# An MLP by seven products on one Trainium2 core: another order of products, three accumulators, other places for the first factors and the last outputs

## The chip, the cores and the metric

The kernel runs on one core of one Trainium2 chip. The metric is the device time of one execution in microseconds; a change of less than about 0.2% can't be told from none.

## The reference

One inference step of a decoder layer for 1024 prompt tokens and 8 samples that share the weights: pooling mixer and gated linear attention in parallel, output projection, cross-attention to memory tokens, and an MLP. The change lies in the MLP and behind it:

```python
    hf = _rmsnorm(x, norm_ffn_g)
    a = jax.nn.relu(jnp.einsum('btd,df->btf', hf, w_up))
    x = x + jnp.einsum('btf,fd->btd', a * a, w_down)
...
    y_prompt = _rmsnorm(xp, norm_final_g)
    y_sample = _rmsnorm(xs, norm_final_g)
```

with D_MODEL = 1024 and D_FF = 4096. All is float32.

## The kernel before

**Arithmetic.** A float32 matrix is split into two parts, `hi` (a cast to fp32r on ScalarE, L157) and `lo` (a subtraction on VectorE, L158), and a matmul is done as three: hi x hi, hi x lo, lo x hi. The two matrix products of the MLP are done by blocks of 2x2, with seven block products in place of eight; the factors are sums and differences of blocks. On the way up a tile m (0 to 15) holds 128 rows of each half of the hidden units. Tokens are in halves of 512 (prompt) and 520 (prompt and samples); products on 520 columns are two matmuls of 260 each.

**Way up.** `first_products(m)` does products 1 and 2 for all 16 m, adds them up, squares the relu, and stores block b11 to DRAM (`fd["2"][m]`); product 1 stays in `P1` (a slot for four m). Then `other_products(m)` does products 4, 6, 5, 7, 3 for each m. Its weights are one tile `w4` (four loads on SyncE, L1131), combined in place on VectorE (L1140 to L1143, `s1` being a tile of its own). Product 7 goes on in the accumulator of product 6, so L1155, which adds `P1` to what stands there, must come before it; product 3 goes on in that of product 5 in the same way (the copy in L1158). L1160 to L1164 add up the results, relu and square follow on ScalarE, and L1172 to L1181 form the factors of the way down, partly in the storage of `w4`; ScalarE and GpSimd store them to DRAM (`fd["1"]`, `fd["3"]` to `fd["7"]`). The b11 block that they need is loaded back (L1135).

**Way down.** `DOWN` lists seven products in the order 2, 3, 1, 6, 5, 4, 7. For each of four m and two halves q, `down_w` loads a weight block (raw `wdn`), splits it into `wdnh` and `wdnl`, `down_part` does the matmuls (L1275), and `factor` loads and splits a factor of the next product, so that eight factors F are there when it begins. For product 2 five factors are made during the loop on the way up (`first_factor`, after m = 2, 4, 5, 9, 13), three at the change to the way down.

**The end.** Product 7 is last. Its last two row blocks are done in column halves (`last_part`); `finish(t)` transposes 128 tokens, takes the norm (L1315, square and sum on ScalarE) and scales (L1318) and stores; the last two token blocks (`ys`, `junk`, `last_sum`) are normed piece by piece, with a last scaling in L1409.

**What sets the order.** A scheduler puts the instructions in order, engine by engine, from the dependences and from the program's order as priority; every engine then runs its list in order, and DMA issues on a queue go in order too. Buffers come from pools: `slot()` gives one of 19 shared slots of a tile pool S (`w4`, `P1`, the split inputs T, F, X), `T()` one of four temporary buffers (`c12` with b11, `c2`, `fac`, `y`), `wp` the raw weights and their split parts. The eight PSUM banks hold two single-bank tiles `mp` and two accumulators of three banks each on the way up; on the way down `mp` has two and `accp` three of two banks. A tile that gets a buffer waits for the last user of the tile that had it.

Of the kernel before, what the change touches and what calls it, by code (L numbers as in the profile page):

```python
# [16 lines left out]
P = 128  # L17
# [43 lines left out]
def body(ctx, tc, a, o):  # L61
# [11 lines left out]
    mp = front.enter_context(tc.tile_pool(name="mp", bufs=2, space=PSUM))  # L73
    accp = front.enter_context(tc.tile_pool(name="accp", bufs=2, space=PSUM))
# [110 lines left out]
    def gemm_steps(src, X, name, cols=ALL):  # L185

        W = src if isinstance(src, list) else load_w(src, name)
        acc = accp.tile([P, NG, 512], F32, tag="acc", name="acc")
# [62 lines left out]
    def tokens_sum(ss, name):  # L251

        pt = accp.tile([P, NG, 512], F32, tag="acc", name="pts")
# [102 lines left out]
    def x_chunk(k):  # L356
        xT = T("xT")
        acc = accp.tile([P, NG, 512], F32, tag="acc", name="ptx")
# [20 lines left out]
    def f_part(k):  # L379
        if k == 0:  # L380
            FW.append(accp.tile([P, NG, 512], F32, tag="acc", name="accf"))
        for j in range(2):
            for g in range(NG):
                PE.matmul(FW[KC][:, g, :GS], FW[k], H[k][j][:, g * GS:(g + 1) * GS],
                          start=(k == 0 and j == 0), stop=(k == KC - 1 and j == 1))
# [70 lines left out]
    def forget():  # L456
# [3 lines left out]
        for p in range(2):  # L460
            acc = accp.tile([P, NG, 512], F32, tag="acc", name="accz")
# [57 lines left out]
    def pool_out(gi):  # L519
# [6 lines left out]
        acc = accp.tile([P, NG, 512], F32, tag="acc", name="accp")  # L526
# [119 lines left out]
    def gla1(c):  # L646
        cs = slice(c * P, (c + 1) * P)
        acc = GA[c] = accp.tile([P, NG, 512], F32, tag="acc", name="accg")
# [297 lines left out]
    def scores(h, tt):  # L946
        acc = accp.tile([P, NG, 512], F32, tag="acc", name="accsc")
# [22 lines left out]
    def context(h, tt):  # L970
        pT = PT.pop((h, tt))
        acc = accp.tile([P, NG, 512], F32, tag="acc", name="accpv")
# [53 lines left out]
    def norm(half):  # L1026
# [3 lines left out]
        pt = accp.tile([P, NG, 512], F32, tag="acc", name="pts3")  # L1030
# [83 lines left out]
    def first_products(m):  # L1114
        acc = accp.tile([P, NG, 512], F32, tag="acc", name="acc12")
# [11 lines left out]
    def other_products(m):  # L1127
# [6 lines left out]
        G.memset(b11[:, HA:], 0.0)  # L1134
        SY.dma_start(b11[:, :HA], fd["2"][m])  # L1135
# [14 lines left out]

        d = mp.tile([P, 512], F32, tag="m", name="acc4")
        product([(d, 0, HA)], w_split(w4[:, 3]), "4")
        va, ta = both(accp.tile([P, NG, 512], F32, tag="acc", name="acc67"))
        product(ta, w_split(w4[:, 0]), "6")
        V.tensor_tensor(out=g2(c12), in0=va, in1=g2(p1), op=ALU.add)  # L1155
        vc, tc_ = both(accp.tile([P, NG, 512], F32, tag="acc", name="acc53"))
        product(tc_, w_split(s1), "5")
        A.copy(out=g2(c22), in_=vc)  # L1158
# [25 lines left out]
    run(ATTN)  # L1184
    for half in range(2):
# [15 lines left out]
    def first_factor(j):  # L1201

        ff = slot([P, 2, 2, HA], F32R, "F2")
        for k in range(2):
            t = wp.tile([P, HA], F32, tag="raw", name="fac2", bufs=3)
            SY.dma_start(t, fd["2"][2 * j + k])
            split(ff[:, 0, k], ff[:, 1, k], t)
        F.setdefault("2", []).append(ff)

    for m in range(MU):  # L1210
        other_products(m)
        if m in (2, 4, 5, 9, 13):
            first_factor(len(F.get("2", [])))
# [9 lines left out]
    mp = ctx.enter_context(tc.tile_pool(name="mpd", bufs=2, space=PSUM, reuse_waits="tile"))  # L1223
    accp = ctx.enter_context(tc.tile_pool(name="accpd", bufs=3, space=PSUM, reuse_waits="tile"))
# [14 lines left out]
    def factor(n, j):  # L1239

        w = width(n)
        t = T("fac", 2 * w).rearrange("p (k n) -> p k n", k=2)
        SY.dma_start(t, fd[n][2 * j:2 * j + 2].rearrange("k p n -> p k n"))
        ff = slot([P, 2, 2, w], F32R, "F" + n)
        split(ff[:, 0], ff[:, 1], t)
        F.setdefault(n, []).append(ff)

    def down_w(n, blocks, op, m, q, keep=False):

        raw = []  # L1250
# [9 lines left out]
        if keep:  # L1260
            w = slot([P, 2, UK, P], F32R, "wd")
            hi, lo = w[:, 0], w[:, 1]
        else:
            hi = wp.tile([P, UK, P], F32R, tag="whi", name="wdnh", bufs=2)
# [175 lines left out]
```

## Time and profile before

| | |
|---|---|
| time, median of 3 runs | 1395.98 us (1395.47 to 1396.54) |
| the profiled execution, its own time | 1395.87 us |
| span, first to last instruction | 1394.2 us |
| TensorE busy | 1328.1 us (95%) |
| VectorE busy | 918.6 us (66%) |
| ScalarE busy | 578.9 us (42%) |
| GpSimd busy | 135.3 us (10%) |
| mean granted TensorE clock | 0.983 |

Busy time leaves out what an engine spends on register, branch, semaphore and DMA-issuing instructions. The span is some 1.7 us shorter than the execution's own time; the latter is compared with the median. The granted clock is a share of full speed, 2.4 GHz; 0.50 is the lower of its two levels, 1.2 GHz.

### The profile page before, as it was taken

The page shows a single profiled execution, that of the slowest core. Times are in us where ns is not written, and L with a number is a line of the kernel's source. Part 1 is how long each engine was busy: PE and PEld are TensorE (multiplying, and loading weights), DVE is VectorE, ACT ScalarE, POOL GpSimd, SP SyncE. Part 2 cuts the span into 40 slices and gives each one's busy share as a digit, 9 for nine tenths or more (in the row PEclk, how much of TensorE's full clock was granted, in tenths as well). Part 3 has the DMA queues.
Part 4 walks back from the last instruction along what each step waited for, and adds up shares of the span by engine and source line. Part 5 has one row for each costly group of instructions (what it writes and reads, how often), then busy time and mean ns, then how long its engine had stood idle before and what let it go on. Part 6 is the DMA issues. An engine that isn't in the chain of part 4 may idle for free. (4 is left out here: it accounts for less than half of the span.)

```text
span 1394.2 us, 22629 instructions
## 1 busy us (share of the span) xinstructions
PE 1328.1 (95%) x8734; PEld 1234.6 (89%) x8734; DVE 918.6 (66%) x1495; ACT 578.9 (42%) x1065; POOL 135.3 (10%) x177
## 2 busy tenths in 40 slices
PE   6999999899999999999999999999979999999996
PEld 6999999888999998878967899889877999989886
DVE  5777565786555687863777587777776555665663
ACT  6522111455344344543466445344454433232522
POOL 2143100100022000002200011211120000000000
PEclk9999999999999999999999999999999999999998
DMA  8846543584455356664435646565659865886661
GB/s 266 261 119 184 156 144 99 159 260 160 148 187 178 102 182 198 199 225 150 132 110 174 184 164 198 182 201 188 204 176 382 279 205 157 265 255 181 231 193 61
DMA packets 287558, 261.39 MB, mean 187 GB/s; under 512 B 13496, under 2 KB 239682, under 8 KB 287321
## 3 DMA queue, kind: packets, MB, share of 16 engines
q1 hardware_dynamic: 275289, 226.08, 52.3%
q0 software_dynamic: 6400, 21.17, 4.1%
q10 hardware_dynamic: 5760, 12.68, 2.5%
q8 instruction: 69, 1.13, 0.3%
q14 instruction: 40, 0.33, 0.1%
HBM read 195.04 MB, written 64.85 MB: 186 GB/s over the span
## 5 line engine op out<-in xcount | busy, mean ns | idle before, releaser
L1107 PE MATMUL acc<-T,wuph 128*128 128x260 f32 (+1 forms) x1408 | 287.9, 316 | 14.7 <-DVE c L1155 10.9
L1275 PE MATMUL accd<-F,wdnh 128*128 128x260 f32 (+1 forms) x1344 | 266.1, 310 | 6.4 <-ACT wdnh L157 6.4
L1107 PEld LDWEIGHTS acc<-T,wuph 128*128 128x128 f32 x1408 | 213.6, 190 | 35.5 <-ACT c L1158 9.0
L1275 PEld LDWEIGHTS accd<-F,wdnh 128*128 128x128 f32 x1344 | 200.9, 189 | 20.6 <-ACT wdnh L157 7.0
L1107 PE MATMUL acc<-T,wupl 128*128 128x260 f32 (+1 forms) x704 | 180.1, 316 | 2.5 <-DVE wupl L158 2.5
L1275 PE MATMUL accd<-F,wdnl 128*128 128x260 f32 (+1 forms) x672 | 167.3, 311 | 5.1 <-DVE wdnl L158 5.1
L1107 PEld LDWEIGHTS acc<-T,wupl 128*128 128x128 f32 x704 | 116.0, 190 | 12.3 <-DVE wupl L158 4.0
L1275 PEld LDWEIGHTS accd<-F,wdnl 128*128 128x128 f32 x672 | 109.4, 188 | 14.0 <-DVE wdnl L158 7.1
L157 ACT CAST wdnh<-wdn 128x1024 fp32r<-128x1024 f32 x52 | 54.4, 1050 | 132.6 <-PE accd L1275 128.1
L157 ACT CAST F<-fac 128x1040 fp32r<-128x1040 f32 (+2 forms) x61 | 59.8, 985 | 64.1 <-DMA fac<-fd 52.5
L194 PE MATMUL acc<-c,womh 128*128 128x260 f32 (+2 forms) x384 | 81.3, 322 | 0.1
L158 DVE TENSOR_TENSOR F<-fac,F 128x1040 fp32r<-128x1040 f32 (+2 forms) x61 | 69.0, 1142 | 17.5 <-ACT F L157 16.7
L158 DVE TENSOR_TENSOR wdnl<-wdn,wdnh 128x1024 fp32r<-128x1024 f32 x52 | 63.4, 1220 | 24.1 <-ACT wdnh L157 22.9
L194 PE MATMUL acc<-hm,wqmh 128*128 128x344 f32 x384 | 72.7, 323 | 0.6 <-DVE v L258 0.6
L157 ACT CAST wuph<-w 128x512 fp32r<-128x512 f32 x64 | 38.6, 615 | 64.4 <-PE acc L1107 64.3
L194 PEld LDWEIGHTS acc<-c,womh 128*128 128x128 f32 x384 | 59.3, 188 | 6.6 <-ACT womh L157 0.8
L1111 ACT ACTIVATE c<-c 128x512 f32<-128x512 f32 (+1 forms) x64 | 40.1, 634 | 57.1 <-DVE c L1162 25.8
L194 PEld LDWEIGHTS acc<-hm,wqmh 128*128 128x128 f32 x384 | 61.7, 188 | 1.6 <-DVE v L258 0.9
L1259 DVE TENSOR_TENSOR wdn<-wdn 128x1024 f32<-128x1024 f32 x24 | 29.4, 1225 | 45.0 <-DMA wdn<-in_w_down 44.9
L194 PE MATMUL acc<-c,woml 128*128 128x260 f32 (+2 forms) x192 | 49.5, 320 | 0.0
L158 DVE TENSOR_TENSOR wupl<-w,wuph 128x512 fp32r<-128x512 f32 x64 | 42.5, 683 | 3.3 <-ACT wuph L157 3.3
L1024 POOL TENSOR_TENSOR ss<-ss,sq 128x512 f32<-128x512 f32 (+1 forms) x12 | 18.9, 1573 | 241.3 <-ACT sq L1022 241.3
(402 smaller groups left out, 2571.7 us busy)
## 6 DMA issues: line engine op xcount, KB each, us to landing
wdn<-in_w_down SPq DMA_DIRECT2D x64, 512.0 KB
fac<-fd SPq DMA_DIRECT2D x32, 520.0 KB
w<-in_w_up SPq DMA_DIRECT2D x64, 256.0 KB
ws<-in_w_down SPq DMA_DIRECT2D x48, 256.0 KB
fac<-fd SPq DMA_DIRECT2D x19, 512.0 KB
fd<-w POOLq DMA_DIRECT2D x32, 260.0 KB, 2.6
x<-xd SPq DMA_DIRECT2D x16, 516.0 KB
xd<-x SPq DMA_DIRECT2D x16, 516.0 KB
```

The costliest lines, as they stand in the source:

```text
L157: A.copy(out=dst_hi, in_=src)
L158: (eng or V).tensor_tensor(out=dst_lo, in0=src, in1=f(dst_hi), op=ALU.subtract)
L194: PE.matmul(acc[:, g, :c1 - c0], w, X[k][j][:, c0:c1], start=(k == 0 and i == 0), stop=(k == len(W) - 1 and i == 2))
L1024: eng.tensor_tensor(out=ss2[:, cs], in0=ss2[:, cs], in1=sq, op=ALU.add)
L1107: PE.matmul(acc, w, t[k // 2][:, k % 2, j, c0:c1], start=(first and k == 0 and i == 0), stop=(k == HK - 1 and i == 2), skip_group_check=True)
L1111: A.activation(out=t, in_=t, func=AF.Relu)
L1259: V.tensor_tensor(out=raw[0], in0=raw[0], in1=raw[1], op=op)
L1275: PE.matmul(acc, W[x][:, k, :], ff[:, y, k % 2, c0:c1], start=(q == 0 and k == 0 and i == 0), stop=(q == 1 and k == UK - 1 and i == 2))
```

## The change

- From the end of the attention on, the PSUM pools are opened anew: two single banks `mp` and three accumulators of two banks (before: two of three banks, until the way down).
- `other_products` does its products in the order 6, 5, 4, 7, 3 (before 4, 6, 5, 7, 3), and the load of b11 (with its memset) stands behind product 4.
- The first four factors of product 2 are loaded after m = 3, 7, 11, 15, each with one load of 512 KB to rows of `P1` that have been used, and split with one cast and one subtraction of 128x1024. Before, there were five, each by two loads of 256 KB through raw weight buffers. The S slot of such a factor is asked for only then.
- At the change, the two weight parts W of the first down block are loaded ahead of the other four factors of product 2; these are loaded to raw weight buffers (`fac2`) instead of T buffers. In `down_w` the split parts get their buffers ahead of the raw ones.
- At the end `ys` and `junk` lie in slots instead of T buffers, `finish(0)` comes ahead of the last part (1, 2), and `finish(1)` behind it.

Line numbers of the kernel with the change are two higher from L159 on, and shift again from L1131 on: L1153 there is L1155 of before, L1162 is L1160, L1166 is L1164, L1418 is L1409, and L1133 and L1160 are the loads of L1131 and L1135.

```diff
@@ -70,8 +70,10 @@
     front = ctx.enter_context(ExitStack())
     sm = front.enter_context(tc.tile_pool(name="sm", bufs=2))
     wp = front.enter_context(tc.tile_pool(name="wp", bufs=2))
-    mp = front.enter_context(tc.tile_pool(name="mp", bufs=2, space=PSUM))
-    accp = front.enter_context(tc.tile_pool(name="accp", bufs=2, space=PSUM))
+    front_p = ctx.enter_context(ExitStack())
+    mp = front_p.enter_context(tc.tile_pool(name="mp", bufs=2, space=PSUM))
+    accp = front_p.enter_context(tc.tile_pool(name="accp", bufs=2, space=PSUM))
+    BANKS = NG
 
     def slot(shape, dt=F32, name="slot"):
         return S.tile(shape, dt, tag="s", name=name)
@@ -185,7 +187,7 @@
     def gemm_steps(src, X, name, cols=ALL):
 
         W = src if isinstance(src, list) else load_w(src, name)
-        acc = accp.tile([P, NG, 512], F32, tag="acc", name="acc")
+        acc = accp.tile([P, BANKS, 512], F32, tag="acc", name="acc")
         yield acc[:, :len(cols), :cols[0][1] - cols[0][0]]
         for k in range(len(W)):
             hi, lo = W[k]
...
@@ -1112,7 +1114,7 @@
         A.activation(out=t, in_=t, func=AF.Square)
 
     def first_products(m):
-        acc = accp.tile([P, NG, 512], F32, tag="acc", name="acc12")
+        acc = accp.tile([P, BANKS, 512], F32, tag="acc", name="acc12")
         product([(acc[:, 0, :HA], 0, HA)], load_w(w_up_block(0, 0, m), "wup"), "1")
         if m % 4 == 0:
             P1.append(slot([P, 4, HB], F32, "p1"))
@@ -1131,8 +1133,6 @@
                 SY.dma_start(w4[:, 2 * i + j], w_up_block(i, j, m).rearrange("(k p) c -> p k c", p=P))
         t = T("c12", 2 * HB)
         b11, c12 = t[:, :HB], t[:, HB:]
-        G.memset(b11[:, HA:], 0.0)
-        SY.dma_start(b11[:, :HA], fd["2"][m])
         p1 = P1[m // 4][:, m % 4, :]
         t = T("c2", 2 * HB)
         u3, c22 = t[:, :HB], t[:, HB:]
@@ -1148,14 +1148,16 @@
         def g2(x):
             return x.rearrange("p (g n) -> p g n", g=2)
 
+        va, ta = both(accp.tile([P, BANKS, 512], F32, tag="acc", name="acc67"))
+        product(ta, w_split(w4[:, 0]), "6")
+        V.tensor_tensor(out=g2(c12), in0=va, in1=g2(p1), op=ALU.add)
+        vc, tc_ = both(accp.tile([P, BANKS, 512], F32, tag="acc", name="acc53"))
+        product(tc_, w_split(s1), "5")
+        A.copy(out=g2(c22), in_=vc)
         d = mp.tile([P, 512], F32, tag="m", name="acc4")
         product([(d, 0, HA)], w_split(w4[:, 3]), "4")
-        va, ta = both(accp.tile([P, NG, 512], F32, tag="acc", name="acc67"))
-        product(ta, w_split(w4[:, 0]), "6")
-        V.tensor_tensor(out=g2(c12), in0=va, in1=g2(p1), op=ALU.add)
-        vc, tc_ = both(accp.tile([P, NG, 512], F32, tag="acc", name="acc53"))
-        product(tc_, w_split(s1), "5")
-        A.copy(out=g2(c22), in_=vc)
+        G.memset(b11[:, HA:], 0.0)
+        SY.dma_start(b11[:, :HA], fd["2"][m])
         product(ta, w_split(w4[:, 2]), "7", first=False)
         V.tensor_tensor(out=g2(u3), in0=va, in1=g2(p1), op=ALU.add)
         V.tensor_tensor(out=c22, in0=u3, in1=c22, op=ALU.add)
@@ -1182,6 +1184,10 @@
         G.dma_start(fd["6"][m], b12)
 
     run(ATTN)
+    front_p.close()
+    mp = ctx.enter_context(tc.tile_pool(name="mpd", bufs=2, space=PSUM, reuse_waits="tile"))
+    accp = ctx.enter_context(tc.tile_pool(name="accpd", bufs=3, space=PSUM, reuse_waits="tile"))
+    BANKS = 2
     for half in range(2):
         for c in range(1, KC):
             add_ctx(c, half)
@@ -1198,19 +1204,21 @@
             t_rest(m // 2)
     F = {}
 
-    def first_factor(j):
-
-        ff = slot([P, 2, 2, HA], F32R, "F2")
-        for k in range(2):
-            t = wp.tile([P, HA], F32, tag="raw", name="fac2", bufs=3)
-            SY.dma_start(t, fd["2"][2 * j + k])
-            split(ff[:, 0, k], ff[:, 1, k], t)
-        F.setdefault("2", []).append(ff)
+    def factor_rows(n, j):
+        return fd[n][2 * j:2 * j + 2].rearrange("k p n -> p k n")
+
+    def factor_split(n, t):
+        ff = slot([P, 2, 2, t.shape[2]], F32R, "F" + n)
+        split(ff[:, 0], ff[:, 1], t)
+        F.setdefault(n, []).append(ff)
 
     for m in range(MU):
         other_products(m)
-        if m in (2, 4, 5, 9, 13):
-            first_factor(len(F.get("2", [])))
+        if m % 4 == 3:
+
+            t = P1[m // 4].rearrange("p a n -> p (a n)")[:, :2 * HA].rearrange("p (k n) -> p k n", k=2)
+            SY.dma_start(t, factor_rows("2", m // 4))
+            factor_split("2", t)
 
 
 
@@ -1220,8 +1228,6 @@
     front.close()
     sm = ctx.enter_context(tc.tile_pool(name="smd", bufs=2, reuse_waits="tile"))
     wp = ctx.enter_context(tc.tile_pool(name="wpd", bufs=2, reuse_waits="tile"))
-    mp = ctx.enter_context(tc.tile_pool(name="mpd", bufs=2, space=PSUM, reuse_waits="tile"))
-    accp = ctx.enter_context(tc.tile_pool(name="accpd", bufs=3, space=PSUM, reuse_waits="tile"))
     MD_ = KC // 2
     X = {}
 
@@ -1239,14 +1245,21 @@
     def factor(n, j):
 
         w = width(n)
-        t = T("fac", 2 * w).rearrange("p (k n) -> p k n", k=2)
-        SY.dma_start(t, fd[n][2 * j:2 * j + 2].rearrange("k p n -> p k n"))
-        ff = slot([P, 2, 2, w], F32R, "F" + n)
-        split(ff[:, 0], ff[:, 1], t)
-        F.setdefault(n, []).append(ff)
+        if n == "2":
+            t = wp.tile([P, 2, w], F32, tag="raw", name="fac2", bufs=4)
+        else:
+            t = T("fac", 2 * w).rearrange("p (k n) -> p k n", k=2)
+        SY.dma_start(t, factor_rows(n, j))
+        factor_split(n, t)
 
     def down_w(n, blocks, op, m, q, keep=False):
 
+        if keep:
+            w = slot([P, 2, UK, P], F32R, "wd")
+            hi, lo = w[:, 0], w[:, 1]
+        else:
+            hi = wp.tile([P, UK, P], F32R, tag="whi", name="wdnh", bufs=2)
+            lo = wp.tile([P, UK, P], F32R, tag="wlo", name="wdnl", bufs=2)
         raw = []
         for b in blocks or [None]:
             raw.append(wp.tile([P, UK, P], F32, tag="raw", name="wdn", bufs=4))
@@ -1257,12 +1270,6 @@
             SY.dma_start(raw[-1], src)
         if op is not None:
             V.tensor_tensor(out=raw[0], in0=raw[0], in1=raw[1], op=op)
-        if keep:
-            w = slot([P, 2, UK, P], F32R, "wd")
-            hi, lo = w[:, 0], w[:, 1]
-        else:
-            hi = wp.tile([P, UK, P], F32R, tag="whi", name="wdnh", bufs=2)
-            lo = wp.tile([P, UK, P], F32R, tag="wlo", name="wdnl", bufs=2)
         split(hi, lo, raw[0])
         return hi, lo
 
@@ -1325,6 +1332,7 @@
                 G.memset(X[i, j][:, :, HA:], 0.0)
         SY.dma_start(X[i, j][:, m, :TH[j].stop - TH[j].start], xd[i * MD_ + m][:, TH[j]])
 
+    W = [down_w("2", None, None, 0, q) for q in range(2)]
     while len(F["2"]) < MU // 2:
         factor("2", len(F["2"]))
 
@@ -1336,7 +1344,7 @@
                 x2_load(*j, m)
             acc, to = down_acc(n)
             for q in range(2):
-                down_part(to, n, down_w(n, blocks, op, m, q), q)
+                down_part(to, n, W.pop(0) if W else down_w(n, blocks, op, m, q), q)
                 factor(nxt, todo.pop(0))
             down_add(acc, outs, m)
             if n == "4":
@@ -1357,8 +1365,9 @@
         down_add(acc, outs, m)
     W = {(m, q): down_w(n, blocks, op, m, q, True) for m in (2, 3) for q in range(2)}
     sc = sm.tile([P, 4, 3], F32, tag="fin3", name="sc3", bufs=1)
-    ys = [T("yl", D) for _ in range(2)]
-    junk = T("junk", D)
+    ys = slot([P, 2, D], F32, "yl")
+    ys = [ys[:, t] for t in range(2)]
+    junk = slot([P, D], F32, "junk")
 
     def last_part(g, m):
         acc = mp.tile([P, 512], F32, tag="m", name="accl")[:, :HA // 2]
@@ -1386,9 +1395,9 @@
         for c in (4, 5, 6, 7, 0, 1):
             turn_out(last[t][:, c // 4, c % 4 * P:c % 4 * P + P], 2 + t, c)
     last_sum(0, slice(512, 1024), [last[t][:, 1] for t in range(2)])
+    finish(0)
     last_part(1, 2)
-    for t in range(2):
-        finish(t)
+    finish(1)
     last_part(1, 3)
     for t in range(2):
         turn_out(last[t][:, 0, 2 * P:3 * P], 2 + t, 2)
```

VectorE in the loop, around the passage from one tile's work to the next. In a name such as `w4_9036` the number is that of the tile: before, `c12_8696` is tile m = 5's, `c12_8873` is m = 6's and `w4_9036` is m = 7's.

```order
L1140 TENSOR_TENSOR s1_9045<-w4_9036 128x512
L1162 TENSOR_TENSOR c2_8699<-c2_8699,acc4_8705 128x512
L1164 TENSOR_TENSOR c12_8696<-acc53_8752,c12_8696 128x520
L1174 TENSOR_TENSOR w4_8691<-c12_8696,c2_8699 128x520
L158 TENSOR_TENSOR wupl_8931<-s1_8877,wuph_8930 128x512
L1141 TENSOR_TENSOR w4_9036<-w4_9036 128x512
L1142 TENSOR_TENSOR w4_9036<-s1_9045,w4_9036 128x512
L1172 TENSOR_TENSOR w4_8691<-c2_8699 128x512
L1179 TENSOR_TENSOR w4_8691<-c12_8696,c2_8699 128x520
L1176 TENSOR_TENSOR c2_8699<-c2_8699,c12_8696 128x512
L1181 TENSOR_TENSOR c12_8696<-c12_8696 128x520
L1155 TENSOR_TENSOR c12_8873<-acc67_8899,p1_7287 128x520
```

With the change, `c12_9026` is m = 7's, `c12_9198` is m = 8's and `w4_9529` is m = 10's:

```order
L1164 TENSOR_TENSOR c2_9027<-c2_9027,acc4_9093 128x512
L1140 TENSOR_TENSOR s1_9536<-w4_9529 128x512
L1166 TENSOR_TENSOR c12_9026<-acc53_9063,c12_9026 128x520
L1176 TENSOR_TENSOR w4_9021<-c12_9026,c2_9027 128x520
L1141 TENSOR_TENSOR w4_9529<-w4_9529 128x512
L1174 TENSOR_TENSOR w4_9021<-c2_9027 128x512
L1142 TENSOR_TENSOR w4_9529<-s1_9536,w4_9529 128x512
L1178 TENSOR_TENSOR c2_9027<-c2_9027,c12_9026 128x512
L1181 TENSOR_TENSOR w4_9021<-c12_9026,c2_9027 128x520
L1153 TENSOR_TENSOR c12_9198<-acc67_9205,p1_7512 128x520
L1183 TENSOR_TENSOR c12_9026<-c12_9026 128x520
L160 TENSOR_TENSOR wupl_9267<-w4_9193,wuph_9266 128x512
```

L1140 for a later tile stands ahead of the results' additions here in both; with the change it is that of three tiles ahead instead of two, and it stands so for m = 6, 10 and 14 only, while for other m it stands at other places of a pass. The split for product 4 (`wupl` of `w4_9193`) is now behind the addition L1153.

SyncE's queue at the change to the way down. `c12` is the load of b11 for m = 15, `wsd2` is the weight of product 2, `fd2` and `fd3` are the factors of products 2 and 3.

```order
L1135 DMA c12_10235<-fd2_4263 128x512
L1131 DMA w4_10398<-in_w_up 128x4x128 x2
L1135 DMA c12_10403<-fd2_4263 128x512
L1243 DMA fac_10582<-fd2_4263 128x2x512
L1243 DMA fac_10587<-fd2_4263 128x2x512
L1243 DMA fac_10592<-fd2_4263 128x2x512
L1257 DMA wdn_10603<-wsd2_784 128x1024
L1243 DMA fac_10633<-fd3_4264 128x2x520
L1326 DMA x10_10597<-xd_127 128x512
L1257 DMA wdn_10638<-wsd2_784 128x1024
```

With the change:

```order
L1160 DMA c12_10378<-fd2_4263 128x512
L1252 DMA fac_10615<-fd3_4264 128x2x520
L1252 DMA fac_10644<-fd3_4264 128x2x520
L1270 DMA wdn_10555<-wsd2_784 128x1024
L1270 DMA wdn_10561<-wsd2_784 128x1024
L1252 DMA fac2_10565<-fd2_4263 128x2x512
L1252 DMA fac2_10570<-fd2_4263 128x2x512
L1252 DMA fac2_10575<-fd2_4263 128x2x512
L1252 DMA fac2_10580<-fd2_4263 128x2x512
L1270 DMA wdn_10656<-wsd2_784 128x1024
L1252 DMA fac_10684<-fd3_4264 128x2x520
```

Two loads of weights now stand ahead of the factors of product 2, and two factors of product 3 ahead of those.

ScalarE at the end. `pty` is the accumulator of `finish`, `ptl` and `ptend` those of the last two token blocks.

```order
L1315 ACTIVATE y,sc<-pty 128x1024
L223 ACTIVATE sc<-sc 128x1
L224 ACTIVATE sc<-sc,expb 128x1
L225 ACTIVATE sc<-sc 128x1
L227 ACTIVATE sc<-sc 128x1
L1376 ACTIVATE junk,sc_13458<-ptl 128x384
L1315 ACTIVATE y,sc<-pty 128x1024
L1376 ACTIVATE junk,sc_13458<-ptl 128x384
L223 ACTIVATE sc<-sc 128x1
L1376 ACTIVATE junk,sc_13458<-ptend 128x128
L224 ACTIVATE sc<-sc,expb 128x1
L1376 ACTIVATE junk,sc_13458<-ptend 128x128
```

With the change:

```order
L1322 ACTIVATE y,sc<-pty 128x1024
L225 ACTIVATE sc<-sc 128x1
L226 ACTIVATE sc<-sc,expb 128x1
L227 ACTIVATE sc<-sc 128x1
L229 ACTIVATE sc<-sc 128x1
L1322 ACTIVATE y,sc<-pty 128x1024
L225 ACTIVATE sc<-sc 128x1
L226 ACTIVATE sc<-sc,expb 128x1
L227 ACTIVATE sc<-sc 128x1
L229 ACTIVATE sc<-sc 128x1
L1385 ACTIVATE junk,sc_13434<-ptl 128x384 x2
L1385 ACTIVATE junk,sc_13434<-ptend 128x128 x2
```

The whole of the second `finish` now stands ahead of the squares of the last two token blocks, where its pieces lay between them.

## Rows read from the trace of the kernel before

**Rows 1.** Busy time by stretch: one pass without a hole; the change to the way down.

```profile
core 0: us, PE busy (x) PEld busy (x) DVE busy (x) ACT busy (x) POOL busy (x), PEclk, DMA share, GB/s
...
835.39:849.65 14.26, 14.26 (x111) 13.74 (x109) 10.11 (x16) 7.25 (x14) 2.81 (x6) 1.00 0.67 218
...
1030.00:1047.00 17.00, 10.52 (x80) 9.59 (x79) 11.68 (x16) 8.78 (x12) 3.30 (x8) 0.85 0.73 229
```

**Rows 2.** Waits of TensorE from 830 us to the end.

```profile
PE acc L1107 <- DVE c L1155: 9.3, 6, 1.8
```

**Rows 3.** TensorE in order of time, pieces of the loop.

```profile
819.24 0.63 PE L1107 MATMUL acc<-T,wuph 128*128 128x512 f32 x2
...
822.01 0.64 PE L1107 MATMUL acc<-T,wuph 128*128 128x260 f32 x4
...
873.82 0.72 PE L1107 MATMUL acc<-T,wuph 128*128 128x260 f32 x4 [1.23 <-DVE c L1155]
...
1038.90 0.40 PE L1107 MATMUL acc<-T,wupl 128*128 128x260 f32 x2
```

**Rows 4.** Waits of VectorE in the loop, 831 to 1030 us.

```profile
DVE s L1140 <- DMA w<-in_w_up: 30.8, 11, 3.9
```

**Rows 5.** Waits of SyncE's queue in the loop, 830 to 1030 us.

```profile
SPq L1131 <- DMA fd<-w: 120.0, 16, 13.5
```

**Rows 6.** VectorE in order of time, one pass of the loop.

```profile
882.56 0.69 DVE L1140 TENSOR_TENSOR s<-w 128x512 f32<-128x512 f32 x1 [3.63 <-DMA w<-in_w_up]
...
889.34 0.69 DVE L1155 TENSOR_TENSOR c<-acc,p 128x520 f32<-128x520 f32 x1
```

**Rows 7.** Chain of waits, its transfers: start, us, what.

```profile
877.18 5.29 DMA w<-in_w_up
...
1030.88 4.76 DMA fd<-c
...
1035.76 3.46 DMA fac<-fd
```

**Rows 8.** The page's DMA issues of the stores: count, KB each, median us to landing.

```profile
fd<-w POOLq DMA_DIRECT2D x32, 260.0 KB, 2.6
```

**Rows 9.** TensorE's busy time and granted clock in two stretches.

```profile
core 0: us, PE busy (x), PEclk, DMA share, GB/s
...
891.66:895.08 3.42, 3.42 (x19) 0.50 0.91 265
...
1041.85:1052.09 10.24, 5.69 (x13) 0.50 1.01 375
```

**Rows 10.** Waits of TensorE in the first products, 700 to 735 us.

```profile
PE acc L1107 <- DVE c L1123: 1.3, 2, 0.9
PE acc L1107 <- ACT p L1121: 0.7, 1, 0.7
```

**Rows 11.** TensorE in order of time, start of the way down.

```profile
1045.26 1.22 PE L1275 MATMUL accd<-F,wdnh 128*128 128x512 f32 x2 [5.96 <-ACT wdnh L157]
1047.62 0.79 PE L1275 MATMUL accd<-F,wdnl 128*128 128x512 f32 x1 [1.14 <-DVE wdnl L158]
```

**Rows 12.** ScalarE in order of time, at the change to the way down.

```profile
1042.57 0.64 ACT L1112 ACTIVATE c<-c 128x520 f32<-128x520 f32 x1
...
1044.16 1.05 ACT L157 CAST wdnh<-wdn 128x1024 fp32r<-128x1024 f32 x1
```

**Rows 13.** VectorE in order of time, at the change to the way down.

```profile
1046.36 1.22 DVE L158 TENSOR_TENSOR wdnl<-wdn,wdnh 128x1024 fp32r<-128x1024 f32 x1
```

**Rows 14.** TensorE's last matmuls, and ScalarE at the end.

```profile
1381.63 0.44 PE L1301 MATMUL ptend<-ident,x 128*128 128x128 f32 x2 [0.30 <-DVE x L1369]
...
1383.28 1.02 ACT L1315 ACTIVATE y<-pty 128x1024 f32<-128x1024 f32 x1 [1.44 <-DMA out_y_p<-y]
...
1384.85 0.28 ACT L1376 ACTIVATE junk<-ptend 128x128 f32<-128x128 f32 x1
```

**Rows 15.** VectorE at the end.

```profile
1386.23 0.16 DVE L1400 TENSOR_SCALAR sc<-sc 128x2 f32<-128x2 f32 x1
...
1386.57 1.28 DVE L1318 SCALAR_TENSOR_TENSOR y<-pty,sc,gfin 128x1024 f32<-128x1024 f32 x1
...
1388.40 1.28 DVE L1409 TENSOR_SCALAR yl<-yl,sc 128x512 f32<-128x512 f32 x3
```

More of the change, by code (lines that the diff above doesn't have):

```diff
@@ L251, in tokens_sum @@
     def tokens_sum(ss, name):
-        pt = accp.tile([P, NG, 512], F32, tag="acc", name="pts")
+        pt = accp.tile([P, BANKS, 512], F32, tag="acc", name="pts")
         for g in range(NG):
@@ L357, in x_chunk @@
         xT = T("xT")
-        acc = accp.tile([P, NG, 512], F32, tag="acc", name="ptx")
+        acc = accp.tile([P, BANKS, 512], F32, tag="acc", name="ptx")
         for t in range(NCH):
@@ L380, in f_part @@
         if k == 0:
-            FW.append(accp.tile([P, NG, 512], F32, tag="acc", name="accf"))
+            FW.append(accp.tile([P, BANKS, 512], F32, tag="acc", name="accf"))
         for j in range(2):
@@ L460, in forget @@
         for p in range(2):
-            acc = accp.tile([P, NG, 512], F32, tag="acc", name="accz")
+            acc = accp.tile([P, BANKS, 512], F32, tag="acc", name="accz")
             for g in range(NG):
@@ L525, in pool_out @@
         w2 = wpool[gi]
-        acc = accp.tile([P, NG, 512], F32, tag="acc", name="accp")
+        acc = accp.tile([P, BANKS, 512], F32, tag="acc", name="accp")
         for q, (x, y) in enumerate(((0, 0), (0, 1), (1, 0))):
@@ L647, in gla1 @@
         cs = slice(c * P, (c + 1) * P)
-        acc = GA[c] = accp.tile([P, NG, 512], F32, tag="acc", name="accg")
+        acc = GA[c] = accp.tile([P, BANKS, 512], F32, tag="acc", name="accg")
         qz = qzs[c % 2]
@@ L946, in scores @@
     def scores(h, tt):
-        acc = accp.tile([P, NG, 512], F32, tag="acc", name="accsc")
+        acc = accp.tile([P, BANKS, 512], F32, tag="acc", name="accsc")
         av = acc[:, :2, :].rearrange("p x (y n) -> p (x y) n", y=2)
@@ L971, in context @@
         pT = PT.pop((h, tt))
-        acc = accp.tile([P, NG, 512], F32, tag="acc", name="accpv")
+        acc = accp.tile([P, BANKS, 512], F32, tag="acc", name="accpv")
         for j in range(2):
@@ L1029, in norm @@
             r3.append(sm.tile([P, NT], F32, tag="rbc", name="r3", bufs=1))
-        pt = accp.tile([P, NG, 512], F32, tag="acc", name="pts3")
+        pt = accp.tile([P, BANKS, 512], F32, tag="acc", name="pts3")
         cols = HALVES[half]
```

## The prediction

> **What bounds the kernel now.** I read the stages first, then TensorE's waits, then whoever each wait names. TensorE is busy nearly everywhere, so only its idle stretches can be won. An undisturbed pass of the loop over `other_products` takes 14.26 us with TensorE busy for all of it (VectorE for 10.11); the 17 us around the change to the way down hold 10.52 us of matmuls at a mean granted clock of 0.85 [rows 1].
>
> The loop first. The 128x512 product 4 starts a pass at 819.24; 14 passes later the last matmul ends at 1038.90 + 0.40 = 1039.30 [rows 3]. That is 220.06 us for 14 x 14.26 = 199.6: **20.4 us lost**. The wait named most often is for L1155 (9.3 us from 830 on) [rows 2]: VectorE's addition after product 6, which has to read the accumulator before product 7 goes on in it; one such hole, of 1.23 us, lies at 873.82 [rows 3]. But L1155 is a 0.7 us operation behind others on an in-order engine. VectorE itself waited 30.8 us, eleven times, at L1140, for a `w4` load [rows 4]: at 882.56 for 3.63 us, and L1155 of that pass could only follow at 889.34 [rows 6]. The load was late because SyncE had waited 120.0 us in 16 waits for stores of old tiles [rows 5]: `w4` lives in one of the shared slots, and its last use is as source of the stores of `fd`. After the last issue the load takes 5.29 us [rows 7]. So the ring is store, slot, load, L1140, L1155, TensorE. Besides, the clock fell to 0.50, the lower level, in stretches such as 891.66 to 895.08 after such holes [rows 9]; two of 3.4 us cost 1.7 us each, within the 20.4.
>
> The change to the way down: after the last product (1039.30) TensorE waits 5.96 us for the first `wdnh` and, two matmuls on, 1.14 us for `wdnl` [rows 11]. The clock is at half from 1041.85 to 1052.09 [rows 9], of which (1052.09 - 1045.26 - 1.14) / 2 = 2.8 us are lost. Together **9.9 us**. Behind it stand loads: a store of `fd` (4.76 us), the factor load queued behind it (3.46 us) [rows 7], and on ScalarE and VectorE the epilogue of the last tile and the factors' splits, until the cast at 1044.16 [rows 12] and the subtraction at 1046.36 [rows 13].
>
> The end: TensorE is through at 1381.63 + 0.44 = 1382.07 [rows 14], the last scaling begins at 1388.40 [rows 15]. In between ScalarE waited 1.44 us for an output store, since the `y` of `finish(1)` needed the T buffer of the first [rows 14], and the 1.28 us L1318 stood ahead of the last square root [rows 15].
>
> **The change part by part.**
>
> *Loop.* The order 6, 5, 4, 7 gives L1153 (the former L1155) two products, 2.87 + 2.77 = 5.6 us, instead of one (2.77 is 819.24 to 822.01 [rows 3]; the four long ones share the other 11.49). The third accumulator takes away the wait of the next product 6. Without the early factor slots there are four `w4` tiles in turn instead of three, so a load waits for the stores of a pass earlier; VectorE's order, though, moves L1140 to other places. I walk one pass with VectorE operations 0.61 us apart (eleven steps from 882.56 to 889.34 [rows 6]), in times after the pass's start: in most passes L1140 comes late enough to have its data. For m = 6, 10 and 14 it stands just before L1166 of the tile three earlier (the order shown for the change), so at the end of a pass. There: in that pass the eight operations of the epilogue, which stores are made from, end at +5, a store (0.54 to issue, 2.6 to land [rows 8]) at +8, four loads are issued by +9.8, the last lands 5.29 later [rows 7]: +15, 0.8 us after the next pass has begun. The split for that pass's product 4 is ten operations behind, done at +7, and is wanted at 2.87 + 2.87 + 0.23 = 6.0. So three holes of about 1 to 1.5 us: 4 us stay, 16.4 go. Bounds: nothing of the 20.4 is kept, or half.
>
> The first four factors as one load and one split per four passes: 1.22 us of VectorE like the subtraction in [rows 13] instead of two of 0.7, hidden in its 4 us of slack per pass; no cover, no more than 1.2 us each.
>
> *First products.* TensorE waits 1.3 us for L1123 and 0.7 us for the copy `p`, both readers of an accumulator [rows 10]. A third accumulator should take the first: **-1.3** (0 to -2).
>
> *Where the pools change.* Two 128x512 matmuls no longer lie ahead of a wait in TensorE's order: 2 x 0.23 = **+0.4**.
>
> *Change to the way down.* W's first load no longer stands behind the factors, so its data are there early. What is left ahead of the cast is the relu of the last tile: the add after product 3 (done at E + 1.2, E being the end of products), two ScalarE passes of 0.64 [rows 12], the cast of 1.05 [rows 12]: hi at E + 3.5. VectorE's subtraction stands behind the whole epilogue (E + 3.8) and takes 1.22 [rows 13]: lo at E + 5.0. TensorE loses 3.5 + 0.9 = 4.4 instead of 7.1. The clock will fall again (it fell 2.5 us after the products ended); I take 1.7 us for that, between 0.8 (as short a stretch as at 891.66) and 4 (as long as at 1041.85) [rows 9]. Then the late factors: the second W load waits for product 3, the four factors are queued behind it, the third and fourth wait for a buffer that a W split frees. The last is issued about E + 8.5, lands 3.46 later [rows 7], is cast and subtracted by E + 14.3; it is wanted 42 matmuls of 0.23 after the start, at E + 14.1 to 15.8. Nearly even; 0.4 us for it. Sum 9.9 - 6.5 = **-3.4** (-6 to +2).
>
> By the Trainium skill (Perfetto Trace Analysis, DMA Optimizations), splitting DMAs into smaller chunks may let some start sooner; here two 256 KB loads become one of 512 KB, so the rule speaks against the change. The trace doesn't bear it out: 512 KB of factor took 3.46 us, 256 KB of `w4` 5.29 [rows 7]. By the rule the sum would lose its 3.4.
>
> *End.* With `finish(0)` earlier, `ys` and `junk` out of the T buffers and `finish(1)` ahead of the last products, nothing but the last tile's own work is left: squares (0.28 each for the last [rows 14]), sums, L1400 about 1.5 us after TensorE ends, 1383.6; then the root chain, which took 2.17 us to 1388.40 and waited 0.55 of that for L1318 [rows 15]: 1385.2. **-3.2** (-2 to -4).
>
> Sum: -16.4 - 1.3 + 0.4 - 3.4 - 3.2 = -23.9. The profiled execution took 1395.87, its span and 1.67 us outside; the median is 1395.98, the same. 1395.9 - 23.9 = **1372.0**.
>
> **Rivals.** (B) The loop stays held back: VectorE has the same 19 operations per pass, SyncE's queue now has the `b11` and factor loads ahead of `w4` loads, and L1140 waits in most passes as now. For it: every pass of before had its wait [rows 4]. Against: a fourth slot, and twice the room for L1153. Half the loop's gain: 1380. (C) The factors at the change are late: a load queued behind another takes longer than 3.46 us, as the store's 4.76 shows [rows 7]. At twice 3.46 plus a clock kept low, TensorE waits 5 us more: 1377. (D) Slower: the `b11` load, in order on SyncE, waits for stores of two passes back, and everything behind it waits too. From 23.9 / 16 = 1.5 us more per pass than I count it eats all the gain; at 2 us it gives 1372 + 32 = 1404. For it: stores are what SyncE waited for [rows 5]. Against: such a load is issued in the pass ahead of its use, with 14 us of room.
>
> **How the numbers follow.** Chances: the sum 0.58 (by itself 1367 to 1377), B 0.21, C 0.16, D 0.05. The range 1363 to 1385 reaches below by the bounds of loop and end (16.4 may be 20.4, the clock may stay up) and above over B and C; it leaves out D, B and C together, and a loop with no gain. 0.2% is 2.8 us, about what can be told from no change. Faster: all but D and a few hundredths of B with C, 0.93; same 0.03; slower 0.04.
>
> **What would show it.** Loop: passes of 14.26 us but for three; no wait for L1153; L1140 waiting less than 10 us in all. Change: first down matmul 3.5 us after the last product; a wait for F in the first down product would speak for C. End: the last L1418 about 3 us after TensorE ends. The prediction is wrong if `w4` loads still end the wait before L1140 in most passes, or if TensorE begins to wait for ScalarE's casts.

## The result and the profile after

The kernel with the change takes 1385.76 us (median; 1384.35 to 1386.28), the kernel before, run with it, 1396.01: a ratio of 0.9923 with a 95% interval of 0.9901 to 0.9945. It is faster by 10.2 us, not by 24, and lies 0.8 us above the range.

Where the time went is read from TensorE's waits over the same stretch as in [rows 2] (line, what it waited for: us in total, times, longest):

```profile
PE acc L1109 <- DVE c L1153: 6.1, 3, 2.4
PE accd L1282 <- ACT wdnh L159: 4.5, 2, 3.7
PE accd L1282 <- DVE wdnl L160: 3.4, 4, 1.4
PE acc L1109 <- ACT wuph L159: 2.2, 1, 2.2
PE acc L1109 <- DVE wupl L160: 0.8, 2, 0.4
```

L1153 stops TensorE three times now where L1155 did six times in [rows 2], but longer. The loop cut at the starts of its passes, from m = 1 on, with the busy time of the engines, the granted clock, the share of the DMA engines and GB/s, shows which passes these are:

```profile
core 0: us, PE busy (x) PEld busy (x) DVE busy (x) ACT busy (x) POOL busy (x), PEclk, DMA share, GB/s
806.31:849.16 42.85, 42.85 (x326) 41.26 (x325) 34.98 (x54) 21.47 (x37) 8.63 (x18) 1.00 0.63 213
849.16:867.53 18.37, 16.35 (x110) 14.94 (x109) 14.43 (x23) 6.91 (x13) 2.80 (x6) 0.91 0.52 168
867.53:896.11 28.58, 28.58 (x219) 27.52 (x218) 20.27 (x31) 14.15 (x24) 5.60 (x12) 1.00 0.66 216
896.11:910.39 14.28, 14.28 (x110) 13.75 (x109) 14.12 (x24) 6.78 (x13) 2.81 (x6) 1.00 0.43 149
910.39:932.60 22.21, 17.64 (x111) 15.84 (x109) 14.94 (x24) 7.42 (x14) 2.80 (x6) 0.85 0.56 176
932.60:975.46 42.86, 42.86 (x327) 41.27 (x325) 34.50 (x54) 21.03 (x37) 8.40 (x18) 1.00 0.61 207
975.46:994.27 18.81, 16.35 (x110) 14.87 (x109) 14.83 (x24) 7.32 (x14) 2.80 (x6) 0.91 0.57 177
```

Every one of these passes is at 14.28 us with TensorE busy throughout, but for those of m = 4, 8 and 12: 18.37, 22.21 and 18.81. They lose 16.5 us, of which 9.05 (2.02 + 4.57 + 2.46) are idle and the other 7.5 are matmuls that took longer. Most of that is the granted clock, which fell to the lower level in each:

```profile
core 0: us, PE busy (x), PEclk, DMA share, GB/s
859.27:862.68 3.41, 3.41 (x11) 0.50 0.35 123
920.71:927.54 6.83, 5.93 (x16) 0.50 0.49 176
985.56:988.98 3.42, 3.42 (x9) 0.50 0.48 155
```

Half of TensorE's busy time in these three stretches, 6.4 us, is what the lower level cost (an estimate from these rows). The other 1.1 us fit the six stops themselves: in the run p4 below, with the clock at 1.00, a pass with one stop holds 0.27 us more of busy time than one without.

The passes are the three in which L1140 stands just before L1166. VectorE's wait at L1140 over the loop (in [rows 4] it was 30.8 us, eleven times), and then, for the pass of m = 8, VectorE in order of time:

```profile
DVE s L1140 <- DMA w<-in_w_up: 14.7, 6, 5.0
```

```profile
893.73 0.69 DVE L1140 TENSOR_TENSOR s<-w 128x512 f32<-128x512 f32 x1 [2.02 <-DMA w<-in_w_up]
...
898.81 0.69 DVE L1166 TENSOR_TENSOR c<-acc,c 128x520 f32<-128x520 f32 x1
...
903.19 0.70 DVE L1181 TENSOR_TENSOR w<-c,c 128x520 f32<-128x520 f32 x1
...
915.92 0.69 DVE L1140 TENSOR_TENSOR s<-w 128x512 f32<-128x512 f32 x1 [5.02 <-DMA w<-in_w_up]
916.53 0.69 DVE L1166 TENSOR_TENSOR c<-acc,c 128x520 f32<-128x520 f32 x1
...
920.77 0.69 DVE L1153 TENSOR_TENSOR c<-acc,p 128x520 f32<-128x520 f32 x1
```

Product 3 ended about 910.4. L1166, which needs nothing else, ran at 916.53, since L1140 before it waited 5.02 us for `w4` of m = 10. TensorE went on with products 6 and 5 and then stopped twice, for product 4's weight (its cast stood on ScalarE behind the relu of L1166's result) and for L1153:

```profile
918.46 0.74 PE L1109 MATMUL acc<-T,wuph 128*128 128x512 f32 x2 [2.16 <-ACT wuph L159]
...
921.61 0.99 PE L1109 MATMUL acc<-T,wuph 128*128 128x260 f32 x3 [2.41 <-DVE c L1153]
```

On SyncE's queue the load's first issue, behind the b11 load:

```profile
906.00 0.34 SPq L1160 DMA_DIRECT2D c<-fd  x1
908.78 0.37 SPq L1133 DMA_DIRECT2D w<-in_w_up  x1
```

It waited for the store of L1182; this is the landing of that line's stores, in that pass and then over the loop:

```profile
DMA to landing us min/median/max: 4.6/4.6/4.6
...
DMA to landing us min/median/max: 2.3/2.6/4.6
```

TensorE at the start of the way down and at its last matmuls, which answer to [rows 11] and [rows 14]:

```profile
1041.03 1.22 PE L1282 MATMUL accd<-F,wdnh 128*128 128x512 f32 x2 [3.74 <-ACT wdnh L159]
1042.70 0.80 PE L1282 MATMUL accd<-F,wdnl 128*128 128x512 f32 x1 [0.45 <-DVE wdnl L160]
...
1374.76 0.44 PE L1308 MATMUL ptend<-ident,x 128*128 128x128 f32 x2 [0.30 <-DVE x L1378]
```

And VectorE's last scaling, as in [rows 15]:

```profile
1378.38 1.28 DVE L1418 TENSOR_SCALAR yl<-yl,sc 128x512 f32<-128x512 f32 x3
```

TensorE waits 4.2 us instead of 7.1, and the last scaling begins 3.2 us after TensorE's last matmul instead of 6.3. Both came as forecast.

The spans, 1394.2 and 1384.6, differ by 9.6. Both traces hold the same number of matmuls in each part, and cut by that count the parts are: 1.7 longer in the first 155 us, where nothing was changed; 0.4 longer from there to the first products; first products and pass 0 together 0.6 shorter; passes 1 to 15 of the loop 3.5 shorter; start of the way down 2.9 shorter; the rest of the way down 1.9 shorter (runs with the old way down are 0.8 to 4.2 shorter there too, so nothing shows this to be work of the change); end 2.7 shorter.

### The profile page after: what moved, and what is told of

Same layout as the page of the kernel before. It is cut to its first block, busy times and chain, and to the rows that moved or that the text cites. A ratio compares the mean times of both kernels' runs of the same rounds, so it can differ in the third digit from the quotient of the medians.

```text
span 1384.6 us, 22609 instructions
## 1 busy us (share of the span) xinstructions
PE 1330.3 (96%) x8734; PEld 1237.2 (89%) x8734; DVE 924.0 (67%) x1490; ACT 578.9 (42%) x1060; POOL 135.3 (10%) x177
## 4 chain that ended last, share of the span: by engine, by line
PE 78%; DVE 7%; DMA 6%; issue 4%; ACT 3%; SPq 0%; POOL 0%; DVEq 0%; ACTq 0%; POOLq 0%
PE acc L196 29%; PE accd L1282 20%; PE acc L1109 16%; PE accl L1282 2%; PE accpv L979 1%; PE acck L345 1%; PE accsc L956 1%; DMA fd<-c 1%; DMA fac<-fd 1%; PE accv L732 1%; DMA w<-in_w_up 1%; PE accg L661 1%; PE psv L913 1%; DMA vt<-in_cache_mem_v 1%; DMA wvm<-in_w_vm 1%
## 5 line engine op out<-in xcount | busy, mean ns | idle before, releaser
L1109 PE MATMUL acc<-T,wuph 128*128 128x260 f32 (+1 forms) x1408 | 290.3, 317 | 10.9 <-DVE c L1153 6.1
L159 ACT CAST wdnh<-wdn 128x1024 fp32r<-128x1024 f32 x52 | 54.5, 1050 | 129.4 <-PE accd L1282 112.4
L160 DVE TENSOR_TENSOR F<-fac,F 128x1040 fp32r<-128x1040 f32 (+1 forms) x52 | 63.2, 1231 | 15.0 <-ACT F L159 13.2
L159 ACT CAST F<-fac 128x1040 fp32r<-128x1040 f32 (+1 forms) x52 | 54.5, 1056 | 44.7 <-DMA fac<-fd 37.3
L159 ACT CAST wuph<-w 128x512 fp32r<-128x512 f32 x64 | 39.0, 614 | 56.8 <-PE acc L1109 48.2
```

The source lines that it names most:

```text
L159: A.copy(out=dst_hi, in_=src)
L160: (eng or V).tensor_tensor(out=dst_lo, in0=src, in1=f(dst_hi), op=ALU.subtract)
L1109: PE.matmul(acc, w, t[k // 2][:, k % 2, j, c0:c1], start=(first and k == 0 and i == 0), stop=(k == HK - 1 and i == 2), skip_group_check=True)
```

## The experiments

All times are medians, the ratio is to the kernel before, run beside each. In the table, "loop" is from the first to the last start of the last 1728 matmuls of the way up (16 passes of 108), in each run's trace; 16 passes without a hole make 228. Where the order of products is new (the change, f1, p2, u2, g1), product 6 of pass 0 begins among the last first products, and 0.8 us of these are counted in the loop. "Gap" is from the start of the last matmul of the way up to the first of the way down.

| run | us | ratio (95%) | loop | gap |
|---|---|---|---|---|
| before | 1396.0 | | 248.5 | 6.2 |
| the change | 1385.8 | 0.9923 (0.9901 to 0.9945) | 245.8 | 4.0 |
| f1_late_sums | 1370.4 | 0.9805 (0.9791 to 0.9819) | 231.1 | 4.0 |
| p1_accumulators | 1397.6 | 1.0007 (0.9993 to 1.0020) | 249.2 | 6.9 |
| p2_way_up | 1390.4 | 0.9954 (0.9938 to 0.9971) | 243.8 | 7.4 |
| p3_end | 1393.9 | 0.9981 (0.9967 to 0.9995) | 249.8 | 6.3 |
| b1_late_sums_before | 1372.8 | 0.9838 (0.9815 to 0.9861) | 228.1 | 6.9 |
| p4_first_factors | 1379.2 | 0.9877 (0.9856 to 0.9899) | 232.2 | 6.2 |
| p5_weights_first | 1393.8 | 0.9986 (0.9968 to 1.0003) | 250.5 | 4.0 |
| g1_first_weights_early | 1371.4 | 0.9826 (0.9805 to 0.9848) | 229.9 | 0.1 |
| u1_old_order | 1375.9 | 0.9842 (0.9818 to 0.9867) | 233.8 | 4.2 |
| u2_old_accumulators | 1377.0 | 0.9858 (0.9833 to 0.9882) | 237.0 | 4.0 |
| h1_old_order_late_sums | 1369.2 | 0.9813 (0.9788 to 0.9839) | 228.2 | 4.0 |
| h2_old_order_three_acc | 1367.6 | 0.9794 (0.9771 to 0.9817) | 228.1 | 5.1 |

**f1_late_sums.** In the kernel with the change, `issue_after` puts an operation behind another on its engine, in order alone; nothing waits longer than that. `BEHIND[m]` is the last weight split of tile m (product 3's), kept for m = 4, 8, 12.

```diff
-        V.tensor_tensor(out=s1, in0=w4[:, 2], in1=w4[:, 3], op=ALU.add)
+        with ExitStack() as order:
+            if m - 2 in BEHIND:
+                order.enter_context(tc.issue_after(BEHIND[m - 2]))
+            V.tensor_tensor(out=s1, in0=w4[:, 2], in1=w4[:, 3], op=ALU.add)
...
+        if m % 4 == 0 and m:
+            BEHIND[m] = SPLIT[0].ins
```

> The kernel with the change, and one thing besides: for m = 6, 10 and 14 the weight sums (L1140 to L1143) are queued on VectorE behind the split for product 3 of the tile two earlier, instead of just ahead of L1166 of the tile three earlier. The same operations, loads and buffers. Theory (a late load blocks VectorE where it stands): the passes of m = 4, 8 and 12, which took 18.4, 22.2 and 18.8 us, fall to 14.3 to 15, 14 to 16 us are won, about 1371 us. Rival 1 (VectorE has too much to do in these passes: a factor's split and four tiles' sums come together): the order changes nothing, 1384 to 1387. Rival 2 (the load itself is too late for product 6 of its tile): the hole moves to the pass of m = 6, 10, 14, 1380 to 1386.

1370.4: the theory's number. Fifteen microseconds hang on where three groups of operations stand. TensorE's busy time from 806 to 1020 us, in the same columns as above:

```profile
806.00:1020.00 214.00, 212.88 (x1605) 204.23 (x1604) 175.02 (x274) 104.85 (x182) 42.34 (x89) 1.00 0.61 201
```

One pass of 16.15 is left, where L1140 of m = 11, which was not moved, waits 4.42 us for its load.

**b1_late_sums_before.** The same edge in the kernel before, for every m from 3 on, behind the last split of tile m - 1.

```diff
+            if m > 2:
+                order.enter_context(tc.issue_after(BEHIND[m - 1]))
```

> The kernel before, with one edit in the order alone: from m = 3 on the weight sums (L1140 to L1143) are queued on VectorE behind the split for product 3 of the tile just before, where they stood ahead of the additions of the tile two before. Buffers, accumulators, order of products and loads as before. Theory (all of the loop's loss is a late load that blocks VectorE where it stands): passes of 14.3 us, 14 to 19 us are won, 1377 to 1382. Rival (three w4 tiles are too few, or product 6 alone is too little room for L1155): passes stay near 15.5 us, 1390 or more.

1372.8, below the theory's range: every pass takes 14.26. This one edge, with no other part of the change, wins 22 us (1394.6 for the kernel before beside it), over twice what the change wins. The 20.4 us of the loop were all due to the place of L1140; neither a third accumulator, nor a fourth `w4` tile, nor more room for L1155 was needed.

**p1_accumulators, p2_way_up, p3_end, p4_first_factors, p5_weights_first.** Parts of the change on the kernel before, each with the change's own lines: the pools alone; pools, order of products and first factors together; the end alone; the first factors alone; the weights ahead of the late factors alone.

> The kernel before, with three accumulators of two banks from the end of the attention on and nothing else of the change. Theory: the first products win 1.3 us, and in the loop product 7 waits for L1155 as before, so 1391 to 1395. Rival (the missing accumulator is what holds the loop): 10 us or more are won, 1386 or less.

> The kernel before with all of the change that concerns the way up: accumulators, order of products, place of the b11 load, first four factors through the used products. The change to the way down and the end stay as before (four factors are loaded late instead of three). Theory (the loop has won 2.7 us and the first products 1.3, the rest came from the change to the way down and the end): 1391 to 1394. Rival (the loop won more and the new start of the way down gave it back): 1386 to 1389.

> The kernel before with the end of the change alone: outputs in slots, first finish earlier, second ahead of the last products. Theory: what lies behind TensorE's last matmul falls by 2.7 us, 1393 to 1393.6. Rival (the store's wait is only replaced by another): 1395 to 1396.

> The kernel before with the first four factors through the used products, and nothing else of the change (four factors are loaded late instead of three). VectorE's order then has L1140 ahead of the additions of the tile three before only for m = 6, 10 and 14. Theory: the loop gets what the whole change gives it, all passes 14.3 us but three of 17 to 22, and the fourth late factor costs 1 us: 1389 to 1393. Rival (the accumulators and the order of products are needed too): 1394 or more.

> The kernel before with the change to the way down alone: the two weight parts loaded ahead of the late factors (here three), those through raw weight buffers. Theory: between the last product of the way up and the first of the way down 2.2 us are won, and 0.7 more from the clock: 1392.5 to 1394. Rival (the weights were not what came last): 1395.5 to 1396.5.

The accumulators alone give nothing, less than the theory had. The waits of TensorE in [rows 10] are replaced by one of 2.1 us for the copy `p`, and in the loop it waits no less than before (15.8 us in all against 13.8; the first fence is over 690 to 1100 us, the second is VectorE's wait, as in [rows 4]; L1157 and L1142 there are L1155 and L1140 of before):

```profile
PE acc L1109 <- DVE c L1157: 13.0, 10, 1.8
...
PE acc L1109 <- ACT p L1123: 2.6, 3, 2.1
```

```profile
DVE s L1142 <- DMA w<-in_w_up: 31.9, 11, 3.9
```

The end and the weights first give about what was forecast (2.1 and 0.8 us by the medians, with intervals as wide; the weights' gap is the 4.0 of the change). The first factors alone win 17 us, far below the expected 1389 to 1393: most passes are free, and the three that remain are only 15.58, 16.46 and 14.87. Two things free the others at once, the fourth `w4` tile and the place of L1140, which p4 changes too; no run tells them apart, but b1 shows that the place alone is enough. So the first factors alone beat the whole change, and with accumulators and order added (p2) 11 us are lost again. p2 itself came at 1390.4, between its theory and its rival.

**u1_old_order, u2_old_accumulators.** The whole change with one of these two undone: products 4, 6, 5, 7, 3 and the b11 load in its old place; or two accumulators of three banks until the way down.

> The kernel with the change, but with the order of products 4, 6, 5, 7, 3 and the b11 load ahead of the sums, as before. Theory (the order is what makes a blocked VectorE cost more: with 4 and 6 first, two splits of a pass lie ahead of the late sum and the third only eight operations behind it, with 6, 5, 4 it is ten behind): three passes of 15 to 16.5 us instead of 18 to 22, 1373 to 1378. Rival (three accumulators cost the time, by letting TensorE's work be queued otherwise): 1384 to 1388.

> The kernel with the change, but with two accumulators of three banks until the way down, as before. Theory (the accumulators do nothing in the loop): 1384 to 1388, passes as with the change. Rival (they cost the time): 1373 to 1378.

Either one gives 9 to 10 us back. For the accumulators my theory fell, and the rival's time came: they do nothing in the loop alone, but cost 9 us together with the new order. With two of them the same three passes take 16.46, 16.70 and 16.57 us; over stretches of 18 us with their holes, the clock stays up:

```profile
850.00:868.00 18.00, 16.56 (x123) 1.00 0.56 175
910.00:928.00 18.00, 16.30 (x121) 1.00 0.58 182
970.00:988.00 18.00, 16.43 (x123) 1.00 0.55 171
```

TensorE's waits from 690 to 1100 us show how the stops are cut: in these passes they are holes of at most 0.7 us each, because product 5 of the next tile has to wait for L1166 already, while with three, in the change, TensorE runs on through two products and then stops for 1.6 to 2.4 us at a time.

```profile
PE acc L1109 <- DVE c L1153: 2.0, 3, 0.7
PE acc L1109 <- DVE c L1166: 1.6, 3, 0.6
```

By the traces the three passes differ by 9.7 us in all, and 6.4 of them are the lower clock. That the short holes are what kept the clock up is not shown. p2 has the accumulators and the order of the change, and its pass of m = 4 has nearly the holes of the change's (1.68 and 0.40 us against 1.63 and 0.39); here the clock stayed at 1.00, and the pass is only 0.4 us longer than with two accumulators:

```profile
848.15:865.00 16.85, 14.77 (x110) 1.00 0.60 187
```

Besides, the load was less late: VectorE's longest wait at L1140 is 2.3 us with two accumulators instead of 5.0, both in the pass of m = 8. In the pass before, L1182 was issued 8.1 us after the pass's start with the change and 7.6 with two accumulators, but its store took 4.6 us to land in the one and 2.9 in the other. That one store is 1.7 us of the difference; why it took longer no run tells apart (in p2 it took 4.5).

With the old order (u1) the passes take 17.83, 15.51 and 15.19 us; the holes are 1.8, 1.0 and 0.7 us, one in each, and the clock falls once, after the first. Two splits of the pass (products 4 and 6) then lie ahead of the late L1140, in the same place where the new order has those of 6 and 5; the third, for the product that begins 5.6 us into the pass, is eight operations behind it instead of ten, and the epilogue of the tile before begins 2.2 us earlier (0.55 us into the pass instead of 2.70).

**g1_first_weights_early.** f1 with the first weight part of the way down loaded and split at the end of the loop, in the weight buffers of the way up.

```diff
+    W0 = []
+    for h in range(2):
+        raw = wp.tile([P, HK, P], F32, tag="raw", name="w0", bufs=3)
+        SY.dma_start(raw, wsd["2"][0][:, h * HK:(h + 1) * HK])
...
+        split(hi, lo, raw)
+        W0.append((hi, lo))
...
+                    w = W[k // HK][x][:, k % HK, :] if isinstance(W, list) else W[x][:, k, :]
...
-    W = [down_w("2", None, None, 0, q) for q in range(2)]
+    W = [W0, down_w("2", None, None, 0, 1)]
```

> The kernel with the late sums, and besides the first weight part of the way down loaded and split during the last pass of the way up, in the weight buffers of the way up (two halves of 128x512) instead of the new pool. Theory (the 3.7 us wait at the start of the way down is the cast behind the last relu, and nothing else is late there): 3 to 5 us are won against the late sums alone, 1365.5 to 1367.5. Rival (the second weight part or the late factors are next): the wait moves to the second half of the first down product, 1368 to 1370.5.

1371.4, not below f1, and 0.9 above the rival's range; the wait moved where the rival had it. The way down begins 0.1 us after the way up ends, and then TensorE stops in the second half of the first product, for a factor:

```profile
1031.79 0.79 PE L1298 MATMUL accd<-F,wdnh 128*128 128x512 f32 x1 [6.34 <-ACT F L161]
```

So the late factors come next behind the weights, as the prediction had it; to win here both would have to come earlier, which no run tried.

**h1_old_order_late_sums, h2_old_order_three_acc.** f1 with the old order of products, with two and with three accumulators.

> The change without its order of products and without its accumulators (both as before), and with the sums for m = 6, 10 and 14 queued late. Theory (first factors, weights first and the end give what they give alone, and the loop has no hole): loop -20, change -3, end -2.7, 1368 to 1371, at or below the late sums with the whole change (1370.4). Rival (order and accumulators pay once the sums are out of the way): 1372 to 1376.

> As the one before, but with the three accumulators of the change. Theory: within 1 us of the one before. Rival (the accumulators win 1.3 us in the first products, as forecast): 1.3 us or more below it.

1369.2 and 1367.6, all passes 14.26; the two can't be told apart by their intervals. The rival's gain in the first products is not in the traces: h2 is 0.7 us longer than h1 to the end of pass 0. The second is the best measured, 18 us below the change. Its loop, in the columns of above:

```profile
806.00:1020.00 214.00, 214.00 (x1623) 206.18 (x1622) 176.65 (x276) 106.08 (x184) 42.38 (x89) 1.00 0.63 204
```

## Why the prediction was wrong

**The step that failed** is the price of the three holes: "So three holes of about 1 to 1.5 us: 4 us stay, 16.4 go." The mechanism was right, down to the three passes and the two instructions, and f1 took it away with 1370.4 us as the result, against a sum of 1372. The term was mis-sized: 16.5 us stayed in these passes. Three things are missing in it. Take the pass of m = 8. I let the epilogue of the pass ahead begin at +0.1 and end at +5, while it began at +2.7, because the L1140 there waits too (2.02 us at 893.73), and L1181 ran at +7.1. I took the median landing of a store, 2.6 us [rows 8], where this one took 4.6. Together the four loads could be issued from +12.7 instead of +8, and the last landed not at +15 but at +19.8; the last step of the walk, 7.1 us from the first issue to the last landing, held. Ahead of the passes of m = 4 and 12 the store did take 2.6 us, and the late epilogue (+1.7 and +2.6, behind L1140's waits of 1.06 and 1.92 us) was enough: L1140 ran 2.3 and 2.75 us into them instead of 0.8. And I counted no clock in the holes, where about 6.4 of the 16.5 us are due to the lower level. [Rows 9] had the pattern: in the loop of before the clock fell for 3.4 us after two of its three holes of 1.8 us. Of the signs that I had named for the loop, the passes of 14.26 us but for three came; L1153 was still waited for, and L1140 waited 14.7 us in all, not under 10.

**What the walk was blind to**: it took the change as parts whose gains add up. The order 6, 5, 4 was credited with room for L1153, the third accumulator with a wait less; but at the place where VectorE is blocked, the two let TensorE run on and put the work that it needs next further behind the block, and in the change's trace the clock fell there three times. p4, u1 and u2 show it: leaving out either of the two makes the change 9 to 10 us faster, and adding both to the first factors (p2 against p4) costs 11 us.

**First products**: forecast -1.3. Cut at the end of pass 0, the stretch is 0.6 us shorter with the change and 0.5 in g1, and 0.8 to 1.0 longer in f1, p1, p2, u1 and h2. All seven have the same wait of 2.06 us for the copy `p`; in the five it is followed by 3.4 us at half clock (720.8 to 724.2 in f1), in the change and g1 it is not. The wait for L1123 went, a longer one came; nothing is left of this term on average.

**Loop**: forecast -16.4, measured -3.5 (passes 1 to 15).

**Where the pools change**: forecast +0.4, measured +0.4 to +0.5 (there is a wait of 0.49 us for a cast at 613.79).

**Change to the way down**: forecast -3.4. The gap is 2.2 us shorter, 3.7 idle and then 0.45 (forecast 3.5 and 0.9); the clock was at half for 6.8 us instead of 10.2, and the first 300 matmuls of the way down take 0.7 us less: -2.9. The sign of C, a wait for F in the first down product, did not come. In p5 the cast again follows the relu and the gap is the same 4.0; g1 shows that the factors are next.

**End**: forecast -3.2; 2.7 us less from the last matmuls to the end, in p3 3.4. That stretch was 10.9 to 12.4 us in the kernels with the old end, so the size is uncertain by a microsecond; the store's wait isn't replaced by another.

Of the rivals B was nearest in number (half of the loop's gain, 1380), but not for its reason: L1140 waits six times, not in most passes. The splitting rule (the Trainium skill, Perfetto Trace Analysis, DMA Optimizations) is not borne out here, though no run splits these loads: p4 has them at 512 KB and is 17 us faster, and TensorE waits for none of these four factors in any run.

## What to carry to other kernels

When an in-order engine waits for a load, look at what is queued behind it before giving the load more buffers: an edge in the order that moves work with slack behind work without it cost nothing here and won 22 us alone. Walk such a place with what its neighbours have already lost, not with undisturbed times, and let the range hold the price of a fallen clock for each hole, since holes of one length came with it and without it. Parts of a change that are each harmless can meet at one place: cost them together, and try the parts alone.

## What the runs showed of the hardware

A fall of the granted clock did not follow from the length of one hole. The same wait of 2.06 us in the first products was followed by 3.4 us at 0.50 in five of seven runs; holes of 1.8 us in the loop of before were followed by it twice of three times; the holes of 1.68 and 0.40 us in p2's pass of m = 4 were not, those of 1.63 and 0.39 in the change's were, and p4's single hole of 1.93 was not. With two accumulators (u2), holes of at most 0.7 us left the clock at 1.00 through the whole loop, in the one trace there is. In the change's three passes about 6.4 of 16.5 us lost were clock. A stop costs more than its idle time also at 1.00: p4's three passes, with one hole each, hold 14.53 us of busy time where a pass without one has 14.26. The stores of L1182, 260 KB each, landed after 2.3 to 4.6 us in one loop.
